# Seven-product pairs for three pairs of each output projection and for all of branch b's gate units, with branch a's last four units at the end of the attention

## The chip, the cores and the metric

The kernel runs on one core of one Trainium2 chip. The metric is device time in microseconds; of the kernel before, three runs gave a median of 880.55 us (879.84 to 883.31). The engines are named as in the profile: PE is TensorE's matmul, PEld its weight load, DVE is VectorE, ACT is ScalarE, POOL is GpSimd, SP is SyncE. A DMA is issued from the queue of SP or of POOL.

## The reference

Two layers of a decoder trunk on 512 tokens of 1024 channels, float32. What matters here:

```
h = rmsnorm(x);  u = h @ W_in             # columns: q, k, v, z of branches a, b, c; gates ga, gb, gc
ya, yb, yc = attention of 4 + 6 + 6 heads, each times silu(z)
merged = sigmoid(ga) * (ya @ w_br_a) + sigmoid(gb) * (yb @ w_br_b) + sigmoid(gc) * (yc @ w_br_c)
x = x + merged @ w_out                    # after two layers: a last rmsnorm
```

## The kernel before

**Data.** Activations lie transposed, channels on the 128 partitions and 512 tokens along the row, in eight tiles. For precision every operand is split in a high and a low part, and every product is three matmuls: high x high, low x high, high x low (`mm3`, L128). A *unit* is 128 output columns of a projection from 1024 inputs: 8 x 3 matmuls of 512 columns (`run_unit`).

**Weights.** A *chunk* is half a unit's weights (256 KB) or a branch projection's (192 KB). Its high part is loaded into a slot of ring `wh` (`RINGH`, 10 slots) by a DMA from POOL's queue (L1110); its low part is made in a slot of ring `wl` (`RING`, 7 slots) by a negation of the high part on ACT (L1139) and an accumulating DMA of the same block (L1140). Chunks that are sums of blocks (L1119) are cast on ACT (L1133) and subtracted on DVE (L1135), from raw blocks loaded by SP.

**A pair in seven products** (`pair_steps`). Two units are taken as a 2x2 block product in seven products of half the inputs and half the tokens (a scheme of Strassen and Winograd): 7 x 4 x 3 = 84 matmuls of 256 columns. Products 0, 1, 4 use plain blocks of the weights (forms `B11`, `B21`, `B22`), products 2, 3, 5, 6 use differences of blocks. Of the activations, four sums of tiles are needed, made once by `sums` (L601 to L611) and kept in the tiles of V (`vb`), of the probabilities (`P`) and in `PH`, `PL`. The products accumulate in PSUM banks `a`, `b`, `c`, read between the products by ACT and DVE.

**Order.** The program's text sets the order of items (`step` for TensorE's, `do` for the rest), loads and splits run ahead of them by the rings, and a planner then orders each engine's queue, except after `manual_schedule`, where the text's order holds. PSUM has three banks `mm` (units), four `att` (scores, transposes, products) and one `pv`.

**A layer.** V projections; then 17 rounds over 16 heads. Round h holds: transposes of head h-1 (L503), the items of slot `a<h>` of `plan`, the P x V product of head h-1 (L549), the scores of head h+1 (L438, L439), the items of slot `b<h>`. The slots hold the units of q, k, z and, as soon as branch a's outputs are there, gate units with their branch projection (`m_item`: 24 + 6 matmuls for branch a, 24 + 9 for b). Heads 0 to 3 are branch a's, 4 to 9 branch b's (scores over up to 512 keys, three banks), 10 to 15 branch c's (banded, two banks). A reduction on DVE (L472) reads each score block. After the rounds: units 2 and 3 of branch b alone, then six pairs (branch b from 4, all of c), then the output projection. In layer 0 it is eight single units (`o_item`), each followed by a step of the next layer's V projection (`v_item`); its results are added to x, stored, scaled and split (`split_x`), squared and summed (`square_sum`, additions on POOL). In layer 1 it is 16 half units (`last_item`, 24 matmuls of 256 columns, first all with the first 256 tokens), with the weights of all eight kept on chip; then the final norm of each half (`rms_pe`, `rms_root`, `store_half`).

Of the kernel before, what the change touches and what calls it, by code (L numbers as in the profile page):

```python
# [13 lines left out]
P = 128  # L14
S = 512
D = 1024
L = 2
# [10 lines left out]
RING = 7  # L28
RINGH = 10
# [35 lines left out]
def tile_trunk(ctx: ExitStack, tc: tile.TileContext, xT, wpk, gT, gfT, bfg, snk,  # L65
# [96 lines left out]
    def square_sum(x, k):  # L162
# [9 lines left out]
    def rms_pe(_, tbs=range(4), accs=("acc",)):  # L172
        ps = st["ss"] = pv_bank()
# [358 lines left out]
    def pv_item(l, h, pair):  # L532
# [64 lines left out]
    def sums(l, k):  # L597
        def run():
# [3 lines left out]
            u, v = tmp(), tmp()  # L602
            nc.vector.tensor_tensor(u[:, T0], a[:, T1], b[:, T1], op=ALU.add)
            nc.vector.tensor_tensor(u[:, T1], u[:, T0], a[:, T0], op=ALU.subtract)
            nc.vector.tensor_tensor(v[:, T0], a[:, T0], a[:, T1], op=ALU.subtract)
            nc.vector.tensor_tensor(v[:, T1], b[:, T0], u[:, T1], op=ALU.subtract)
            h, lo = sum_places(k)
            for n, w in ((0, u), (1, v)):
                c = slice(n * S, n * S + S)
                nc.scalar.copy(h[:, c], w)  # L610
                nc.vector.tensor_tensor(lo[:, c], w, rd(h[:, c]), op=ALU.subtract)  # L611
            st["SH", k], st["SL", k] = h, lo
        return run

# [31 lines left out]
    def pair_steps(l, br, i, last=False):  # L646
# [5 lines left out]

        def A(half, tok):
            return lambda k: (XH[k + 4 * half][:, tok], XL[k + 4 * half][:, tok])

        def Sm(m):
            c = slice((m - 1) * HT, m * HT)
            return lambda k: (st["SH", k][:, c], st["SL", k][:, c])

        def prod(bank, form, xf):  # L660
            def pe(HL):
                new = bank not in d
                if new:
                    d[bank] = att_bank()[:, :HT]
                wh, wl = HL[0]
                for k in range(4):
                    c = slice(k * P, (k + 1) * P)
                    xh, xl = xf(k)
                    mm3(d[bank], wh[:, c], wl[:, c], xh, xl, new and k == 0, k == 3,
                        bank != "c")  # L670
            step(pe, [("w", l, br, i, form)])
# [77 lines left out]
        prod("b", 2, Sm(1))  # L749
        do(now(e5))  # L750
        prod("a", 3, Sm(2))
# [4 lines left out]
        prod("b", 4, Sm(4))  # L756
        do(now(c12))
        prod("a", 5, Sm(3))
# [12 lines left out]
    def o_item(e):  # L771
        d = {}

        def pe(HL):
            if e == 0:
                load_res(0)
                load_res(1)
            d["ps"] = run_unit(HL, [st["MH", i] for i in range(8)], [st["ML", i] for i in range(8)], LATE)

        def post():  # L780
            x1 = tmp()
            nc.vector.tensor_tensor(x1, d["ps"], st["xr", e], op=ALU.add)
            if e + 2 < 8:
                load_res(e + 2)
            nc.sync.dma_start(x1d[:, e, :], x1)
            split_x(x1, 1, e)
            square_sum(x1, e)
        step(pe, [("o", 0, e, h) for h in range(2)])
        do(post)

    def load_half(n):
        hf, e = divmod(n, 8)
        t = st["xr", n] = T([P, S], F32, "sz", 2)[:, :HT]
        nc.sync.dma_start(t, x1d[:, e, hf * HT:(hf + 1) * HT])

    def last_item(hf, e):
        d = {}
        n = 8 * hf + e  # L800
        tok = slice(hf * HT, (hf + 1) * HT)

        def pe(HL):
            if n == 0:
                load_half(0)
                load_half(1)
            if hf == 0:
                st["WO", e] = HL
            ps = mm_bank()[:, :HT]
# [7 lines left out]
        def post():  # L817
            if hf == 0:
                st["X2", e] = T([P, S], F32, "mg", 8)
            x2 = st["X2", e][:, tok]  # L820
            nc.vector.tensor_tensor(x2, d["ps"], st["xr", n], op=ALU.add)
            if n + 2 < 16:
                load_half(n + 2)
            acc = f"acc{hf}"
            if e == 0:
                st[acc] = T([P, S], F32, "ys", 2)[:, :HT]
                nc.scalar.activation(st[acc], x2, AF.Square)
            else:
                sq = tmp()[:, :HT]
                nc.scalar.activation(sq, x2, AF.Square)  # L830
                if e < KT - 1:
                    nc.vector.tensor_tensor(st[acc], st[acc], sq, op=ALU.add)
                else:
                    st[f"sq{hf}"] = sq
            nc.scalar.activation(x2, x2, AF.Copy, scale=st["gf"][:, e:e + 1])
        step(pe, [("o", L - 1, e, h) for h in range(2)] if hf == 0 else ())
# [17 lines left out]
    def last_projection():  # L854
        h0, h1 = range(0, 2), range(2, 4)
        for e in range(8):
            last_item(0, e)
            if e == 6:
                do(root_warm)
        for e in range(8):  # L860
            last_item(1, e)
            if e == 1:
                step(lambda _: rms_pe(_, h0, ("acc0", "sq0")))
                do(lambda: rms_root(h0))
            if e == 3:
                step(lambda _: rbc_pe(_, h0))
                do(lambda: store_half(0))
        step(lambda _: rms_pe(_, h1, ("acc1", "sq1")))
# [407 lines left out]
```

## Time and profile before

| | |
|---|---|
| median of three runs | 880.55 us |
| the profiled execution | 884.22 us |
| its span | 882.5 us |
| TensorE busy | 865.5 us, 98% |
| VectorE, ScalarE, GpSimd busy | 64%, 58%, 50% |
| granted clock, mean | 0.994 |

The span is the time from the first to the last instruction of one profiled execution; the runs are timed without a profile. An engine's busy time is a union over its instructions, so pipelined matmuls don't count twice.

### The profile page before, as it was taken

To read this page: it belongs to the slowest core of one execution; us is meant where nothing else is said; L and a number is where in the kernel's file an instruction comes from. 1 tells how busy PE (TensorE), PEld (TensorE's weight loads), DVE (VectorE), ACT (ScalarE), POOL (GpSimd) and SP (SyncE) were. 2 spreads that over 40 slices of the span, in tenths; PEclk is the share of its full clock that TensorE was granted. 3 is DMA by queue.
4 is the path that set the end of the run, shared out by engine and by line. 5 is a ranking of instruction groups with operands and counts; after the bars stand their busy time and mean duration, and the time that the engine had idled before them with its cause. 6 is when DMAs were issued, how large, how long until landed. Compare 5 with 4: busy or idle time off the path is not lost.

```text
span 882.5 us, 14401 instructions
## 1 busy us (share of the span) xinstructions
PE 865.5 (98%) x4866; PEld 750.1 (85%) x4866; DVE 567.9 (64%) x1242; ACT 510.4 (58%) x1072; POOL 440.5 (50%) x570
## 2 busy tenths in 40 slices
PE   9999999999999999999999999999999999999995
PEld 6988888888888889987888888888888888999994
DVE  7446788577576767752124658967685858687633
ACT  7477567565655655554335856666465756556541
POOL 5354576655444254566654446666444434544301
PEclk9999999999999999999999999999999999999997
DMA  9697768978989799999997886888899897998413
GB/s 303 142 207 141 161 142 168 190 144 189 199 182 228 193 185 247 205 200 284 250 233 156 174 164 149 153 168 172 158 205 193 186 223 158 226 247 183 160 48 111
DMA packets 97082, 163.83 MB, mean 186 GB/s; under 512 B 12144, under 2 KB 26864, under 8 KB 97008
## 3 DMA queue, kind: packets, MB, share of 16 engines
q0 software_dynamic: 71424, 121.70, 69.2%
q1 hardware_dynamic: 25440, 41.20, 14.2%
q8 instruction: 38, 0.62, 0.3%
q14 instruction: 36, 0.29, 0.1%
q10 hardware_dynamic: 144, 0.01, 0.0%
HBM read 153.43 MB, written 4.19 MB: 179 GB/s over the span
## 4 chain that ended last, share of the span: by engine, by line
PE 76%; issue 7%; POOL 5%; DMA 5%; DVE 3%; ACT 2%; SPq 0%; POOLq 0%; DVEq 0%; ACTq 0%
PE mm L131 17%; PE mm L130 17%; PE mm L132 17%; PE att L130 3%; PE att L131 3%; PE att L132 3%; PE pv L549 3%; PE att L503 3%; POOL wl L1140 3%; POOL wh L1110 2%; PE att L439 2%; PE att L438 2%; PE att L234 1%; PE att L235 1%; PE att L233 1%
## 5 line engine op out<-in xcount | busy, mean ns | idle before, releaser
L1140 POOL DMA_DIRECT2D wl<-in_wpk_dram x248 | 224.7, 925 | 185.8 <-ACT wl L1139 157.0
L1110 POOL DMA_DIRECT2D wh<-in_wpk_dram x248 | 169.6, 693 | 175.4 <-PE mm L132 130.2
L1139 ACT ACTIVATE wl<-wh 128x512 fp32r<-128x512 f32 (+3 forms) x248 | 148.3, 602 | 141.7 <-PE mm L132 113.2
L130 PE MATMUL mm<-xh,wh 128*128 128x512 f32 x544 | 217.6, 400 | 0.0
L131 PE MATMUL mm<-xl,wh 128*128 128x512 f32 x544 | 214.5, 394 | 0.0
L132 PE MATMUL mm<-xh,wl 128*128 128x512 f32 x544 | 214.4, 394 | 0.0
L132 PEld LDWEIGHTS mm<-xh,wl 128*128 128x128 f32 x544 | 102.2, 188 | 24.1
L130 PEld LDWEIGHTS mm<-xh,wh 128*128 128x128 f32 x544 | 102.3, 188 | 22.2
L131 PEld LDWEIGHTS mm<-xl,wh 128*128 128x128 f32 x544 | 102.3, 188 | 22.1
L474 ACT ACTIVATE P<-P,ng 128x256 f32<-128x256 f32 (+3 forms) x128 | 67.0, 525 | 24.9 <-DVE ng L472 24.4
L130 PE MATMUL mm<-y,wh 128*128 128x512 f32 (+1 forms) x132 | 49.9, 378 | 1.2 <-ACT y L711 1.2
L529 DVE TENSOR_TENSOR PL<-att,PH 128x512 fp32r<-128x512 f32 (+2 forms) x84 | 46.1, 598 | 7.0 <-ACT PH L528 7.0
L131 PE MATMUL mm<-y,wh 128*128 128x512 f32 (+1 forms) x132 | 50.1, 379 | 0.3 <-DVE y L712 0.3
L132 PE MATMUL mm<-y,wl 128*128 128x512 f32 (+1 forms) x124 | 47.5, 383 | 0.0
L130 PE MATMUL att<-xh,wh 128*128 128x256 f32 x144 | 40.7, 282 | 0.0
L492 DVE TENSOR_SCALAR P<-P,den 128x256 f32<-128x256 f32 (+3 forms) x128 | 39.8, 376 | 1.0
L132 PE MATMUL att<-xh,wl 128*128 128x256 f32 x144 | 40.4, 281 | 0.0
L131 PE MATMUL att<-xl,wh 128*128 128x256 f32 x144 | 40.4, 281 | 0.0
L528 ACT CAST PH<-att 128x512 fp32r<-128x512 f32 (+2 forms) x84 | 38.8, 526 | 1.3 <-PE att L503 0.6
L439 PE MATMUL att<-qk,qk 128*128 128x256 f32 (+2 forms) x128 | 36.9, 308 | 0.0
L503 PE MATMUL att<-ident,P 128*128 128x128 f32 x284 | 36.2, 272 | 0.0
L438 PE MATMUL att<-qk,qk 128*128 128x256 f32 (+2 forms) x128 | 36.1, 308 | 0.0
(260 smaller groups left out, 2034.8 us busy)
## 6 DMA issues: line engine op xcount, KB each, us to landing
wh<-in_wpk_dram POOLq DMA_DIRECT2D x196, 256.0 KB, 4.7
wl<-in_wpk_dram POOLq DMA_DIRECT2D x196, 256.0 KB, 5.2
y<-in_wpk_dram SPq DMA_DIRECT2D x32, 256.0 KB, 5.5
qk<-in_wpk_dram SPq DMA_DIRECT2D x24, 256.0 KB, 4.8
wh<-in_wpk_dram POOLq DMA_DIRECT2D x32, 192.0 KB, 5.0
wl<-in_wpk_dram POOLq DMA_DIRECT2D x32, 192.0 KB, 4.4
tmp<-tmp SPq DMA_DIRECT2D x80, 64.0 KB, 4.0
mg<-in_xT_dram SPq DMA_DIRECT2D x8, 256.0 KB, 5.7
```

The lines of the kernel that those rows point to most:

```text
L130: nc.tensor.matmul(ps, wh, xh, start=first, stop=False, skip_group_check=part)
L131: nc.tensor.matmul(ps, wh, xl, start=False, stop=False, skip_group_check=part)
L132: nc.tensor.matmul(ps, wl, xh, start=False, stop=last, skip_group_check=part)
L438: nc.tensor.matmul(ps, q[:, qs], kh[:, a:a + n], start=True, stop=False)
L439: nc.tensor.matmul(ps, q2[:, qs], k2[:, a:a + n], start=False, stop=True)
L474: nc.scalar.activation(pb, pb, AF.Exp, bias=ng[:, i:i + 1], scale=-1.0, accum_out=den[:, i:i + 1])
L492: nc.vector.tensor_scalar(blks[i], blks[i], den[:, i:i + 1], None, op0=ALU.mult)
L503: nc.tensor.transpose(ps[:, c * P:(c + 1) * P], pt[:, src * P:(src + 1) * P], st["ident"])
L529: nc.vector.tensor_tensor(st["PL"][:, o:o + n], bk[:, :n], rd(hh), op=ALU.subtract)
L1110: nc.gpsimd.dma_start(hl[i][0][:, :w], ap)
L1139: nc.scalar.activation(lo[:, :w], rd(h[:, :w]), AF.Copy, scale=-1.0)
L1140: nc.gpsimd.dma_start(lo[:, :w], ap, accum_op=ALU.add)
```

## The change

It makes seven-product pairs of all eight gate units of branch b (four pairs a layer, before two) and of six of the eight output units of each layer. In layer 0 output units 0 and 1 stay single and the pairs (2,3), (4,5), (6,7) alternate with V steps; in layer 1 units 6 and 7 stay as half units, first tokens ahead of the pairs and last tokens behind them. Four sums of the merged tiles (`sums_m`, with the body of `sums` in `four_sums`) are made for them; product 6 goes to the bank of `pv`, and layer 1 loads its eight residual tiles into `xh`, `xl` (`residuals`). The squares of layer 0's projection are added on DVE (`side`). Branch a's gate units move later: 0 to 3 are spread over slots a6 to a14, 4 and 5 stand in the last slots and 6 and 7 behind the rounds, where branch b's units stood. The rings shrink, since two more tiles hold branch outputs. All pieces of layer 0's output pairs are split on chip from raw blocks (`is_split`).

```diff
-RING = 7
-RINGH = 10
+RING = 6
+RINGH = 8
...
-            eng = nc.vector if k == KT - 1 else nc.gpsimd
+            eng = nc.vector if k == KT - 1 else side
...
-                yh, yo = (y_slot((2 * pair + w) % 10) for w in range(2))
+                yh, yo = (y_slot(2 * pair + w) for w in range(2))
...
+    def four_sums(k, a, b):
+        u, v = tmp(), tmp()
+        nc.vector.tensor_tensor(u[:, T0], a[:, T1], b[:, T1], op=ALU.add)
+        nc.vector.tensor_tensor(u[:, T1], u[:, T0], a[:, T0], op=ALU.subtract)
+        nc.vector.tensor_tensor(v[:, T0], a[:, T0], a[:, T1], op=ALU.subtract)
+        nc.vector.tensor_tensor(v[:, T1], b[:, T0], u[:, T1], op=ALU.subtract)
+        h, lo = sum_places(k)
+        for n, w in ((0, u), (1, v)):
+            c = slice(n * S, n * S + S)
+            nc.scalar.copy(h[:, c], w)
+            nc.vector.tensor_tensor(lo[:, c], w, rd(h[:, c]), op=ALU.subtract)
+    def sums_m(k):
+        return lambda: four_sums(k, st["M", k], st["M", k + 4])
...
+    def o_pair(l, e, bank, res, finish):
+        def add(u, tok, b, first):
+            def run():
...
+                other = st["xr", e + u] if first else x[u]
+                nc.vector.tensor_tensor(x[u][:, tok], d[b], other[:, tok], op=ALU.add)
+                if not first:
+                    finish(e + u, x[u], tok)
+            return urgent(run) if l + 1 < L else run
+        res(e)
+        prod("a", 0, M(0, T0))
+        do(add(0, T0, "a", True))
+        prod("c", 1, M(1, T0))
+        do(add(0, T0, "c", False))
+        prod("b", 2, sum_part(1))
+        do(add(1, T1, "b", True))
+        prod("a", 3, sum_part(2))
+        do(add(1, T0, "a", True))
+        prod("b", 4, sum_part(4))
+        do(add(1, T0, "b", False))
+        prod("a", 5, sum_part(3))
+        do(add(1, T1, "a", False), add(0, T1, "a", True))
+        prod("e", 6, M(1, T1))
+        do(add(0, T1, "e", False))
+    def first_projection():
...
+        do(lambda: load_res(0), lambda: load_res(1), sums_m(0))
+        o_item(0)
+        do(sums_m(1))
+        o_item(1)
+        do(sums_m(2), sums_m(3))
+        o_pair(0, 2, mm_bank, res, finish)
+        v_item(1, 0)
+        v_item(1, 1)
+        o_pair(0, 4, mm_bank, res, finish)
+        v_item(1, 2)
+        v_item(1, 3)
+        o_pair(0, 6, mm_bank, res, finish)
+        for k in range(4, 8):
+            v_item(1, k)
...
     def last_projection():
+        do(residuals, sums_m(0), sums_m(1))
+        last_item(T0, 6)
+        do(root_warm, sums_m(2))
+        last_item(T0, 7)
+        do(sums_m(3))
+        for e in (0, 2, 4):
+            o_pair(1, e, att_bank, lambda e: None, finish)
+        do(lambda: ctx.enter_context(tc.manual_schedule()))
+        step(lambda _: rms_pe(_, h0, ("acc0", "sq0"), att_bank))
+        do(lambda: rms_root(h0))
+        last_item(T1, 6)
+        step(lambda _: rbc_pe(_, h0))
+        do(lambda: store_half(0))
+        last_item(T1, 7)
...
-            "b5": [(0, 0)], "a6": [(0, 1)], "b7": [(0, 2)], "b8": [("qc", 1, 12)], "a9": [("qc", 2, 14)],
-            "b9": [(0, 3)], "a10": [(0, 4)], "b10": [("zc", 0, 5)], "a11": [(0, 5)], "b11": [],
-            "a12": [(0, 6)], "a14": [("zc", 2, 7)], "a15": [(0, 7)], "a16": [(1, 0)], "b16": [(1, 1)],
+            "b5": [], "a6": [(0, 0)], "b7": [], "b8": [], "a9": [("qc", 1, 12)],
+            "b9": [], "a10": [(0, 1)], "b10": [], "a11": [("zc", 0, 5)], "b11": [("qc", 2, 14)],
+            "a12": [(0, 2)], "a14": [(0, 3)], "a15": [("zc", 2, 7)], "a16": [(0, 4)], "b16": [(0, 5)],
...
-        solo(M(1, 2))
+        solo(M(0, 6))
         do(sums(l, 1))
-        solo(M(1, 3))
-        for br, i in ((1, 4), (1, 6), (2, 0), (2, 2), (2, 4), (2, 6)):
+        solo(M(0, 7))
+        for br, i in ((1, 0), (1, 2), (1, 4), (1, 6), (2, 0), (2, 2), (2, 4), (2, 6)):
...
+    def is_split(key):
+        return is_plain(key) or key[0] == "w" and (key[4] in SUMS or key[1:3] == (0, 3))
```

The slots of `plan` stand here several to a line; slots that are not named keep what they hold.

## Rows read from the trace of the kernel before

**Rows 1.** The page, parts 1 and 2: busy time; 40 slices in tenths.
```profile
PE 865.5 (98%) x4866; PEld 750.1 (85%) x4866; DVE 567.9 (64%) x1242; ACT 510.4 (58%) x1072; POOL 440.5 (50%) x570
...
PEclk9999999999999999999999999999999999999997
DMA  9697768978989799999997886888899897998413
```

**Rows 2.** TensorE's waits: engine, line, releaser: us in total, times, longest.
```profile
PE att L130 <- ACT tmp L721: 2.8, 2, 1.5
...
PE mm L130 <- ACT y L711: 1.2, 2, 0.7
```

**Rows 3.** Stretches: length; busy (count) of PE, PEld, DVE, ACT, POOL; clock, DMA share, GB/s.
```profile
282.20:305.17 22.97, 22.97 (x102) 18.59 (x100) 16.62 (x33) 14.43 (x26) 9.46 (x14) 1.00 0.91 217
319.61:333.71 14.10, 14.10 (x103) 13.31 (x102) 9.12 (x16) 7.12 (x15) 7.09 (x10) 1.00 0.95 191
390.29:391.71 1.42, 1.42 (x13) 1.42 (x12) 0.33 (x1) 1.05 (x2) 1.11 (x3) 1.00 1.18 264
431.92:437.47 5.55, 5.55 (x25) 4.50 (x24) 0.00 (x0) 1.23 (x2) 3.65 (x5) 1.00 0.96 231
822.05:851.93 29.88, 28.88 (x243) 28.48 (x242) 15.23 (x29) 17.30 (x35) 7.77 (x6) 1.00 0.30 94
```

**Rows 4.** Timeline at transposes and scores: start, us, engine, line, op, out<-in, count.
```profile
149.48 1.25 PE L503 MATMUL att<-ident,P 128*128 128x128 f32 x10
150.49 0.48 PE L130 MATMUL mm<-xh,wh 128*128 128x512 f32 x1
...
142.52 0.39 PE L130 MATMUL mm<-xh,wh 128*128 128x512 f32 x1
...
143.46 0.07 DVE L472 DVE_READ_ACCUMULATOR2_ANT ng<- 128x1 f32 x1
143.94 0.07 DVE L472 DVE_READ_ACCUMULATOR2_ANT ng<- 128x1 f32 x1
...
174.89 0.39 PE L130 MATMUL mm<-xh,wh 128*128 128x512 f32 x1
...
175.91 0.08 DVE L472 DVE_READ_ACCUMULATOR2_ANT ng<- 128x1 f32 x1
177.09 0.07 DVE L472 DVE_READ_ACCUMULATOR2_ANT ng<- 128x1 f32 x1
```

**Rows 5.** Timeline of one chunk of a gate pair: negation, accumulating DMA, first use.
```profile
331.82 0.53 ACT L1139 ACTIVATE wl<-wh 128x384 fp32r<-128x384 f32 x1 [0.64 <-PE att L132]
...
332.64 0.87 POOL L1140 DMA_DIRECT2D wl<-in_wpk_dram  x1
...
340.79 0.40 PE L130 MATMUL mm<-y,wh 128*128 128x512 f32 x1
```

**Rows 6.** Gate pairs, 305 to 391: tiles wl, then wh; ScalarE's waits.
```profile
DMA to landing us min/median/max: 3.5/5.1/7.4
...
DMA to landing us min/median/max: 3.0/5.6/7.7
...
ACT wl L1139 <- DMA wh<-in_wpk_dram: 7.1, 6, 1.8
```

**Rows 7.** Timeline of VectorE in the sums: two of 256 columns, two of 512.
```profile
305.66 0.41 DVE L605 TENSOR_TENSOR tmp<-tmp 128x256 f32<-128x256 f32 x1
306.00 0.41 DVE L606 TENSOR_TENSOR tmp<-tmp,tmp 128x256 f32<-128x256 f32 x1
306.33 0.68 DVE L611 TENSOR_TENSOR vb<-tmp,vb 128x512 fp32r<-128x512 f32 x1
306.94 0.68 DVE L1135 TENSOR_TENSOR wl<-qk,wh 128x512 fp32r<-128x512 f32 x1
```

**Rows 8.** The stretch in which the first projection's sums would be made.
```profile
388.39:407.00 18.61, 18.11 (x82) 14.21 (x81) 7.58 (x13) 8.81 (x17) 12.51 (x18) 1.00 1.12 254
```

**Rows 9.** Timeline of VectorE: scaling half of the output, at the end.
```profile
874.45 2.08 DVE L851 TENSOR_TENSOR tmp<-pv,mg 128x256 f32<-128x256 f32 x6 [1.30 <-ACT rbc L841]
```

More of the change, by code (lines that the diff above doesn't have):

```diff
@@ L160, in split_x, with square_sum @@
                                            op0=ALU.mult, op1=ALU.subtract)
-    def square_sum(x, k):
+    def square_sum(x, k, side=nc.gpsimd):
         if k == 0:
@@ L601, in run, with part, sum_part, products @@
                 nc.scalar.activation(t, t, AF.Copy, scale=g_sb[:, l, kk:kk + 1])
[L602 to L612, printed above, removed]
-        return run
+            four_sums(k, a, b)
+        return run
+    def four_sums(k, a, b):
[9 more added lines that the diff above has]
+            nc.vector.tensor_tensor(lo[:, c], w, rd(h[:, c]), op=ALU.subtract)
+        st["SH", k], st["SL", k] = h, lo
+    def sums_m(k):
+        return lambda: four_sums(k, st["M", k], st["M", k + 4])
+    def part(hs, ls, half, tok):
+        return lambda k: (hs[k + 4 * half][:, tok], ls[k + 4 * half][:, tok])
+    def sum_part(m):
+        c = slice((m - 1) * HT, m * HT)
+        return lambda k: (st["SH", k][:, c], st["SL", k][:, c])
+    def products(key, d, new_bank):
+        def prod(bank, form, xf):
+            def pe(HL):
+                new = bank not in d
+                if new:
+                    d[bank] = (pv_bank if bank == "e" else new_bank)()[:, :HT]
+                wh, wl = HL[0]
+                for k in range(4):
+                    c = slice(k * P, (k + 1) * P)
+                    xh, xl = xf(k)
+                    mm3(d[bank], wh[:, c], wl[:, c], xh, xl, new and k == 0, k == 3, bank not in "ce")
+            step(pe, [key + (form,)])
+        return prod
     def m_item(l, br, i):
@@ L651, in pair_steps @@
         now = urgent if br == 2 else (lambda fn: fn)
+        prod = products(("w", l, br, i), d, att_bank)
         def A(half, tok):
[L654 to L671, printed above, removed]
+            return part(XH, XL, half, tok)
         def branch(u):
@@ new lines, in first_projection, with res, run, finish @@
+    def first_projection():
+        def res(e):
+            def run():
+                for u in range(2):
+                    if e == 4:
+                        t = T([P, S], F32, "sz", 2)
+                    else:
+                        t = y_slot(8 + u, F32)
+                    st["xr", e + u] = t
+                    nc.sync.dma_start(t, xT[:, e + u, :])
+            do(run)
+        def finish(e, x1, tok):
+            if tok == T0:
+                return
+            nc.sync.dma_start(x1d[:, e, :], x1)
+            split_x(x1, 1, e)
+            square_sum(x1, e, nc.vector)
+        do(lambda: load_res(0), lambda: load_res(1), sums_m(0))
[12 more added lines that the diff above has]
+            v_item(1, k)
@@ new lines, in quarter @@
+    def quarter(e, x, tok, last):
+        hf = int(tok == T1)
+        x2 = x[:, tok]
+        acc = f"acc{hf}"
+        if acc not in st:
+            st[acc] = T([P, S], F32, "ys", 2)[:, :HT]
+            nc.scalar.activation(st[acc], x2, AF.Square)
+        else:
+            sq = tmp()[:, :HT]
+            nc.scalar.activation(sq, x2, AF.Square)
+            if last:
+                st[f"sq{hf}"] = sq
+            else:
+                nc.vector.tensor_tensor(st[acc], st[acc], sq, op=ALU.add)
+        nc.scalar.activation(x2, x2, AF.Copy, scale=st["gf"][:, e:e + 1])
```

164 lines of the change are left out of this document (66 added, 98 removed).

## The prediction

> **What bounds the kernel now.** I read the page first, then TensorE's waits, then tables of stretches cut at the first matmul of an item, and last the timelines of the places that the change touches. [rows 1] TensorE is busy 98% of 882.5 us, in every slice, with its clock granted in full (2.4 GHz), while VectorE stands at 64%. [rows 2] Its longest waits are 2.8 and 1.2 us in total, so no other engine holds it: the kernel lasts as long as TensorE's work, plus the start and the tail. Two questions follow: how much TensorE work goes, and which engines, covered today, are covered no longer.
>
> **What is removed.** [rows 3] Three single units of branch b (99 matmuls of 512 columns) take 22.97 us, 7.66 each and 15.31 for two. A pair in seven products with its two branch projections takes 14.10. One product (12 matmuls of 256 columns) takes 1.42, a single output unit (24 of 512) 5.55, a half output unit (24 of 256) twice 1.42, or 2.84.
> - Branch b: units 0 to 3 of each layer become two pairs, so four pairs in all: 4 x (15.31 - 14.10) = 4.8 us.
> - First output projection: three pairs, 3 x (2 x 5.55 - 7 x 1.42) = 3 x 1.16 = 3.5 us.
> - Last output projection: its units run as halves already, so a pair replaces four halves: 3 x (4 x 2.84 - 9.94) = 4.3 us.
> - [rows 3] The last stretch, 240 matmuls, takes 29.88 us where 20 x 1.42 = 28.4 are needed: it waits 1.5 us for the last merged channels; such waits stand in [rows 2]. After the change the first halves there need only the first 256 tokens, which are merged earlier; I count 1.3 (0 to 1.5).
> Sum 13.9 us. Branch a's last units move and cost the same 30 matmuls each.
>
> One rule speaks against all of this. The rows give 0.118 us a matmul of 256 columns and 0.231 of 512: halving the width halves the time. The Trainium skill (TensorE: Matmul & The Clock Gate, "Back-to-back issue gap") has about 81 ns sustained for 128 columns and 131 for 512; an estimate from that page for 256 is some 98 ns, by which seven products (84 x 98 = 8.2 us) would cost 1.9 us more than the 48 wide matmuls (6.3 us) and the change would lose some 10 us. The trace disagrees on both widths, so this rule gets no chance.
>
> **What is added.** Five costs; none of them is matmul work.
>
> (a) Attention, thinner cover. Per layer the sixteen heads lose two units of branch a and two of branch b, so slots b5, b7, b8, b9 and b10 are empty while heads 4 to 9 still use three score banks and three transpose banks out of four. With nothing between the scores of head h+1 and the transposes of head h, the second transpose bank waits for the second reduction and the third for the third. [rows 4] Ten transposes take 1.01 us. Scores that end at 142.52 have their second reduction done at 143.53 and the third at 144.01: 0.4 us of transposes, 0.6 of waiting, 0.4, then 0.1; 0.7 us lost. Scores that end at 174.89 have theirs at 175.99 and 177.16: 0.7 + 0.8 = 1.5 us. Three such places a layer (b5, b7, b8; at b9 and b10 the next head needs two banks): six in all, 4.2 to 9.0 us. The lower end is 0: the planner may put the next unit's matmuls, which wait for nothing, ahead of the transposes. I take 2.5, a little over half of 4.2.
>
> (b) Weight rings, low parts 7 to 6, high parts 10 to 8. [rows 5] A low part in the pairs is made by a negation on ScalarE (331.82), an accumulating DMA issued 0.8 us later (332.64) and used at 340.79, 9.0 us after the negation, which starts when the slot comes free. [rows 6] The DMA lands after 5.1 us in the median and 7.4 at most: the chain needs 5.9, at most 8.2. With six slots the negation starts five chunks before the use: 7.1 us where these are five products, 7.8 to 8.4 where branch projections of (14.10 - 9.94) / 2 = 2.08 are among them. So only the slowest landings are late, by 1.1 us. In 16 pairs I count one or two: 1.5 us. Bounds 0 (fewer transfers in flight may land sooner) and 16, worked out under the rivals.
>
> (c) Sums for the first projection. The three pairs need four sums of the merged channels: 16 VectorE operations of 256 columns and 8 of 512. [rows 7] Back to back these start 0.34 and 0.60 us apart, so 4 x 2.56 = 10.2 us. From the last gate pair's second branch projection (388.39) to the last sum's use is 3.3 us to the end of that pair, 11.1 of two single units, 2.84 of two products and 1.06 of the third: 18.3 us, about the stretch to 407. [rows 8] VectorE is busy 7.6 of 18.6 us there and has 11.0 free. New in it: sums 10.2, splits of the first four forms 3.6, a squares addition that was GpSimd's 0.6, two additions 0.7: 15.1, less 2.7 for the first two sums' additions, which need channels merged a pair earlier. That is 12.4 in 11.0: 1.4 late, of which 0.2 may hide; I take 1.2. Bounds 0 (matmuls of the next layer's v units put ahead) and 5 (nothing done early, and an us of waits for ScalarE between).
>
> (d) Sums for the last projection. Here only two half units (5.68) precede the products: from the same point 3.5 + 5.68 + 2.84 + 1.06 = 13.1 us. VectorE owes the last pair's merging (4.1), sums 10.2, splits of two forms 2.4, two residual additions with their squares 1.0, two additions 0.7: 18.4 - 2.7 = 15.7, 2.6 late. Behind them the three pairs give no recovery: each asks VectorE for 8 x 0.60 + 12 x 0.34 = 8.9 us in 9.94. And ScalarE casts between the steps. I take 3.3; bounds 1 (additions and later splits put off) and 8 (a tenth of VectorE's 40 us here lost to in-order waits, and the residuals, now loaded only when their slots come free after the last gate product, late).
>
> (e) Tail. The first half's scaling now lies between the last two half units. [rows 9] Six products take 2.08 us; with the addition, square and accumulation of the unit before them (1.6 us after its last matmul) they end 3.7 us after that matmul, where the last unit's addition could start at 3.2: 0.4 us. Bounds 0 and 1.5, the latter if the root's chain is late too.
>
> Sum added 2.5 + 1.5 + 1.2 + 3.3 + 0.4 = 8.9. Net -5.0. The profiled execution took 884.22 us, 1.8 of them around its span, and would take 879.2; it lies 3.67 above the median of the runs, 880.55, so the forecast there is **875.5 us**.
>
> What costs nothing: fewer bytes move in the first projection (a pair's four blocks are loaded once and split on chip); [rows 1] the DMA engines stay the busiest thing beside TensorE in the gate pairs, as before. SP's loads of raw blocks stand ahead of the residuals in program order, so the residuals wait, not the weights.
>
> **Rivals.**
> - **The waits stay hidden.** The planner fills (a) and (c) with other matmuls, the rings hold, (d) costs its lower bound. For it: [rows 2] today's order leaves hardly any wait in 880 us. Against: in the last projection no other matmul is ready. 13.9 - 0.4 - 1.0 = 12.5 saved: 868.0 us.
> - **VectorE becomes the bound in both projections**: (c) 5 and (d) 8, the rest as forecast: 17.4 added, +3.5: 884.0 us. For it: the demand over the last projection (18.4 and 3 x 8.9 against 39 us of TensorE's) is above the time. Against: [rows 8] half of VectorE's time at this place is free today.
> - **The rings decide, and it gets slower.** A high part's slot is held from its load to its last matmul: [rows 6] 5.6 to land, 0.8, 5.1, then 1.42 of use, 12.9 us. A pair uses nine chunks in 14.10, 1.57 each: ten slots give 15.7 us, eight give 12.5. Short by 0.4 in eight chunks, 0.45 a pair, 7.2 in 16 pairs; with a slowest landing in every second pair 8 x 1.1 = 8.8: 16.0 for (b) instead of 1.5. +9.5: 890.0 us. It decides from the point where a slot's tour is longer than eight chunks. For it: [rows 6] ScalarE already waits 7.1 us in six waits for high parts to land, with ten slots. Against: four of nine chunks are cast from blocks on chip and hold their slots shortly.
>
> **How the numbers follow.** Forecast 0.45 (its own range 872 to 880), hidden waits 0.24, VectorE 0.20, rings 0.11. The range runs from 867, where nothing but the smallest of the costs is left, to 889, which leaves out most of the ring case's far side. What a measurement of this kernel can tell is some 0.5%, 4.4 us, so faster is below 876.1: all of the hidden case and over half of the forecast, 0.48. Slower is above 885.0: the rings and a part of VectorE's case, 0.19. Same 0.33.
>
> **What would show it.** After the change TensorE's busy time falls by 12 to 13 us; pairs of units take 9.9 us in the projections and 14.1 in branch b. Waits of TensorE on VectorE at the transposes of heads 5, 7 and 8, and at the third product of the first pair of each projection, show (a), (c) and (d); waits on an accumulated weight in the gate pairs show (b). The prediction is wrong if those at the third products are absent, if gate pairs are longer than 14.5 us, or if TensorE's idle time exceeds 25 us.

## The result, and the profile after

The changed kernel takes 945.51 us (median of 4 runs, 943.73 to 949.96) against 880.69 for the kernel before on the same chip: a ratio of 1.074, 95% interval 1.069 to 1.078, so 65 us slower. The forecast was 875.5, its range ended at 889. The profiled execution took 943.73 us, its span 942.0. One execution of a kernel of the experiments, e4, took 4820 us where its other three took about 910; the times given for it leave that one out.

The page of the changed kernel, the lines of [rows 1]:
```profile
PE 877.3 (93%) x5082; PEld 760.5 (81%) x5082; DVE 644.1 (68%) x1423; ACT 537.1 (57%) x1132; POOL 418.1 (44%) x550
...
PEclk9999999999999999989999999999999999999898
DMA  8497777679999899875497877775798998889862
```
TensorE now idles 65 us of the span, 17 before. Its busy time was to fall by 12 to 13 us and rose by 11.8; the lower clock explains some 10 of that difference (last section), the rest wasn't traced. Its longest waits, the view of [rows 2]:
```profile
PE att L132 <- DMA wl<-in_wpk_dram: 17.1, 19, 2.1
PE att L503 <- DVE ng L472: 6.2, 4, 3.0
PE mm L132 <- DMA wl<-in_wpk_dram: 5.6, 6, 1.8
PE att L130 <- DVE tmp L751: 4.9, 1, 4.9
PE att L130 <- ACT P L614: 3.4, 1, 3.4
PE att L234 <- DMA wl<-in_wpk_dram: 3.0, 1, 3.0
```
Low parts (wl) that the accumulating DMA hasn't delivered, the attention's transposes (L503), and the sums of the third product (L614) all show now. Where the time went is read from the stages, with the columns of [rows 3]: attention, gate pairs and first projection of layer 0, then attention, gate pairs and last projection of layer 1. Before:
```profile
41.78:305.17 263.39, 263.39 (x1318) 221.30 (x1316) 182.50 (x431) 166.09 (x366) 139.41 (x177) 1.00 0.85 182
305.17:391.71 86.54, 84.99 (x613) 79.74 (x612) 62.18 (x112) 48.30 (x95) 46.14 (x66) 1.00 0.94 199
391.71:459.69 67.98, 67.48 (x290) 53.93 (x289) 15.39 (x24) 26.98 (x45) 44.11 (x58) 1.00 1.09 256
472.42:735.75 263.33, 263.33 (x1318) 221.18 (x1317) 183.25 (x431) 166.08 (x367) 139.62 (x177) 1.00 0.86 180
735.75:822.05 86.30, 84.97 (x613) 79.75 (x612) 64.44 (x114) 47.88 (x95) 40.08 (x54) 1.00 0.91 206
822.05:873.90 51.85, 48.71 (x406) 47.82 (x404) 24.15 (x58) 24.47 (x52) 9.21 (x8) 0.98 0.27 87
```
After:
```profile
42.54:283.07 240.53, 235.42 (x1185) 195.87 (x1184) 174.18 (x423) 159.65 (x355) 123.80 (x155) 1.00 0.82 174
283.07:412.45 129.38, 118.28 (x817) 108.05 (x816) 81.27 (x147) 59.26 (x119) 57.34 (x80) 0.99 0.89 198
412.45:489.32 76.87, 68.28 (x398) 57.91 (x397) 52.74 (x101) 35.86 (x62) 20.09 (x29) 0.96 0.68 163
503.04:743.40 240.36, 235.70 (x1185) 197.08 (x1183) 172.77 (x422) 158.08 (x353) 123.27 (x155) 0.99 0.80 172
743.40:877.67 134.27, 118.57 (x818) 108.31 (x817) 83.04 (x151) 61.44 (x124) 61.34 (x87) 0.98 0.91 206
877.67:934.00 56.33, 48.18 (x369) 46.24 (x368) 43.45 (x105) 31.44 (x66) 11.11 (x16) 0.95 0.57 149
```
The attention lost four units of 7.66 us, so 232.7 were due and each takes 8 more. Eight gate pairs at the 14.4 us each of before are 115: they take 14 and 19 more. The first projection was due at 68.0 - 3.5 = 64.5 and takes 12 more; the last with its tail at 51.9 - 5.6 = 46.3 and takes 10 more. No stage gained what it was to gain.

Behind the gate pairs stands ScalarE: its negations now wait for high parts to land (the line of [rows 6], over the whole span; the kernel before, then the changed one):
```profile
ACT wl L1139 <- DMA wh<-in_wpk_dram: 13.2, 12, 1.8
...
ACT wl L1219 <- DMA wh<-in_wpk_dram: 105.4, 44, 5.4
```
The longest, 5.4 us, falls on the start of the first projection. Timeline of ScalarE and VectorE there (start, length, engine, line, what, and idle time before with its releaser):
```profile
415.58 0.63 ACT L1219 ACTIVATE wl<-wh 128x512 fp32r<-128x512 f32 x1 [5.37 <-DMA wh<-in_wpk_dram]
416.12 1.12 ACT L614 CAST vb<-tmp 128x512 fp32r<-128x512 f32 x2
...
416.75 1.29 DVE L615 TENSOR_TENSOR vb<-tmp,vb 128x512 fp32r<-128x512 f32 x2 [5.49 <-ACT vb L614]
...
419.40 0.62 ACT L725 CAST y<-mg 128x512 fp32r<-128x512 f32 x1 [1.63 <-DVE mg L714]
```
One negation waits for one landing. Behind it in ScalarE's order stand the sums' casts; VectorE idles 5.5 us for those, adds up the last merged channels only after them, and ScalarE casts these at 419.40, while TensorE waits. Two-microsecond stretches of the same place (columns as above):
```profile
414.00:416.00 2.00, 1.87 (x9) 1.17 (x7) 0.00 (x0) 0.42 (x1) 0.00 (x0) 1.00 1.08 272
416.00:418.00 2.00, 0.33 (x1) 0.30 (x2) 1.25 (x3) 1.77 (x4) 1.42 (x2) 1.00 1.08 298
418.00:420.00 2.00, 0.88 (x4) 0.38 (x2) 1.66 (x4) 0.60 (x2) 0.00 (x0) 0.70 1.11 241
420.00:422.00 2.00, 1.93 (x3) 0.78 (x3) 1.95 (x5) 1.36 (x4) 0.00 (x0) 0.50 0.52 145
422.00:424.00 2.00, 1.52 (x4) 1.12 (x4) 1.97 (x5) 0.75 (x2) 0.00 (x0) 0.50 0.00 0
424.00:426.00 2.00, 2.00 (x7) 1.58 (x6) 2.00 (x6) 1.29 (x3) 0.00 (x0) 0.59 0.12 44
```
After some 3 us with little to do TensorE's clock stands at 0.50 (1.2 GHz) until 424 and later, and most of the wait is paid a second time.

### The profile page after: what moved, and what is told of

It reads as the page before. It is cut to its first block, busy times and chain, and to the rows that moved or that the text cites. A ratio compares the mean times of both kernels' runs of the same rounds, so it can differ in the third digit from the quotient of the medians.

```text
span 942.0 us, 15134 instructions
## 1 busy us (share of the span) xinstructions
PE 877.3 (93%) x5082; PEld 760.5 (81%) x5082; DVE 644.1 (68%) x1423; ACT 537.1 (57%) x1132; POOL 418.1 (44%) x550
## 4 chain that ended last, share of the span: by engine, by line
PE 46%; DMA 18%; issue 14%; POOL 9%; DVE 7%; ACT 4%; SPq 1%; POOLq 0%; DVEq 0%; ACTq 0%
PE mm L130 10%; PE mm L132 10%; PE mm L131 10%; DMA wh<-in_wpk_dram 7%; DMA wl<-in_wpk_dram 6%; POOL wl L1220 5%; POOL wh L1189 4%; PE att L503 3%; PE pv L549 3%; DMA tmp<-tmp 3%; PE att L132 2%; PE att L130 2%; PE att L131 1%; PE att L438 1%; PE att L439 1%
## 5 line engine op out<-in xcount | busy, mean ns | idle before, releaser
L1219 ACT ACTIVATE wl<-wh 128x512 fp32r<-128x512 f32 (+3 forms) x241 | 143.4, 600 | 199.3 <-DMA wh<-in_wpk_dram 105.4
L130 PE MATMUL mm<-xh,wh 128*128 128x512 f32 x480 | 193.1, 402 | 0.0
L132 PE MATMUL mm<-xh,wl 128*128 128x512 f32 x480 | 190.5, 397 | 0.0
L131 PE MATMUL mm<-xl,wh 128*128 128x512 f32 x480 | 189.9, 396 | 0.0
L132 PE MATMUL att<-xh,wl 128*128 128x256 f32 x192 | 57.0, 297 | 14.8 <-DMA wl<-in_wpk_dram 14.7
L131 PE MATMUL att<-xl,wh 128*128 128x256 f32 x192 | 54.7, 285 | 0.0
L132 PEld LDWEIGHTS att<-xh,wl 128*128 128x128 f32 x192 | 37.2, 194 | 18.3 <-DMA wl<-in_wpk_dram 18.1
L503 PE MATMUL att<-ident,P 128*128 128x128 f32 x284 | 38.9, 275 | 8.9 <-DVE ng L472 6.2
L130 PE MATMUL att<-vb,wh 128*128 128x256 f32 x152 | 43.8, 288 | 1.8 <-ACT tmp L735 1.6
L503 PEld LDWEIGHTS att<-ident,P 128*128 128x128 f32 x284 | 32.3, 141 | 15.9 <-issue 9.1
L132 PE MATMUL att<-vb,wl 128*128 128x256 f32 x152 | 43.5, 286 | 1.7 <-DMA wl<-in_wpk_dram 1.7
L130 PE MATMUL mm<-y,wh 128*128 128x512 f32 (+1 forms) x106 | 41.9, 395 | 1.7 <-ACT y L725 1.7
L131 PE MATMUL att<-vb,wh 128*128 128x256 f32 x152 | 43.2, 284 | 0.0
```

Of the source, the lines that this page charges most:

```text
L130: nc.tensor.matmul(ps, wh, xh, start=first, stop=False, skip_group_check=part)
L131: nc.tensor.matmul(ps, wh, xl, start=False, stop=False, skip_group_check=part)
L132: nc.tensor.matmul(ps, wl, xh, start=False, stop=last, skip_group_check=part)
L503: nc.tensor.transpose(ps[:, c * P:(c + 1) * P], pt[:, src * P:(src + 1) * P], st["ident"])
L1219: nc.scalar.activation(lo[:, :w], rd(h[:, :w]), AF.Copy, scale=-1.0)
```

## The experiments

Each kernel was timed beside the kernel before (882 to 884 us in these sessions); ratios are to that, with 95% intervals. "Six and eight" are six low and eight high slots.

**Rings.** e1, the kernel before with the change's rings; e2 and e3, the changed kernel with one slot more:
```
e1:  RING = 7, RINGH = 10  ->  RING = 6, RINGH = 8     (kernel before)
e2:  RING = 6              ->  RING = 7                (changed kernel)
e3:  RINGH = 8             ->  RINGH = 9               (changed kernel)
```


> The kernel before with the change's rings alone: six slots for low parts instead of seven, eight for high parts instead of ten; all else as before (the last projection's resident weights that lose their ring slots get tiles of their own in the freed space). Theory DMA (my own now): in the gate pairs the 16 DMA engines have more to move than time. Per pair 2.36 MB on GpSimd's queues at 18.62 MB in 72.2% of 129.38 us (199 GB/s) and 1.05 MB on SyncE's at 6.82 MB in 16.0% (329 GB/s): 11.8 + 3.2 = 15.0 us of all engines, 16.0 at the 0.94 share that the gate pairs of before reach, against 14.1 of TensorE. Then the rings only set how much is loaded ahead: losing two high and one low parts costs at most 3 x 1.3 = 4 us a layer, so 881 to 889. Rival, rings: a slot's tour sets the pace and the changed kernel's 2.0 to 2.7 us per gate pair come from the smaller rings; the twelve pairs of before lose as much: 25 us or more, 905.

> The changed kernel with seven low slots again (high parts stay at eight). Rings theory: the low parts are what TensorE waits for in its gate pairs (16.1 us in 17 waits in the two layers), so with the slot back at least half of the 38 us go: 927 or less. DMA theory: the engines still have 16 us of work per pair; one chunk more of reserve is worth 1.5 us a layer: 941 to 946.

> The changed kernel with nine high slots (low parts stay at six). Rings theory with the high slot's tour (12.9 us against eight chunks 12.5; nine give 14.1): the pace recovers, 38 us go but for some: 915. DMA theory: one chunk of reserve, 1.5 us a layer: 941 to 946.

Measured: e1 915.04 us (1.036, 1.034 to 1.039), e2 1018.21 (1.152), e3 921.58 (1.042). My theory, bytes, fell three times: e1 lost 33 us where 881 to 889 us was forecast, and one slot more costs 73 us in the low ring and gives 24 in the high one. e1's gate pairs and first projection of layer 0:
```profile
308.62:402.74 94.12, 87.04 (x613) 79.84 (x612) 61.10 (x110) 46.02 (x93) 42.97 (x61) 1.00 0.84 177
402.74:477.01 74.27, 71.02 (x291) 55.72 (x290) 15.74 (x24) 27.31 (x46) 45.63 (x60) 0.95 1.05 238
```
Against 86.54 and 67.98 before, with a DMA share that is lower, not higher (0.84 against 0.94). ScalarE's wait for high parts in e1, whose rings differ by two, and in e2, where they differ by one:
```profile
ACT wl L1140 <- DMA wh<-in_wpk_dram: 80.0, 37, 3.7
...
ACT wl L1219 <- DMA wh<-in_wpk_dram: 295.8, 137, 6.5
```
In e3, with a difference of three, it is 23.5 us. So I formed a second theory, lead: only the difference of the rings counts, since the negation is issued that many chunks behind its load.
```
e5:  RING = 6  ->  RING = 5                      (changed kernel)
e6:  RING = 7  ->  RING = 6                      (kernel before)
e9:  RING = 7, RINGH = 10 -> RING = 6, RINGH = 9 (kernel before)
```


> The changed kernel with five low slots instead of six, so less room, but three chunks instead of two between the load of a high part and its negation (eight less five). Theory lead: the negations stand in ScalarE's order and wait for a high part that was asked for only as many chunks earlier as the two rings differ; a chunk is 1.57 us in the gate pairs, a landing 5.8 us, so two chunks (3.1 us) make nearly every negation wait and three (4.7 us) few. Sums of these waits so far: difference three 13.2 us (before) and 23.5 (six and nine), two 105.4 (the change) and 80.0 (before with six and eight), one 295.8 (seven and eight). So ScalarE's wait on high parts falls from 105 to 20 to 35 us and the time to 921, as with six and nine; 915 to 932 since five low slots leave the accumulation 6.3 us instead of 7.8. Rival, capacity: fewer slots are worse, and what helped with nine was the slot: 950 to 965.

> The kernel before with six low and ten high slots: difference four. Theory lead: the 13.2 us of ScalarE's waits on high parts go nearly to nothing; TensorE hardly waited for them, so 878 to 884, no loss from the low slot. Rival, capacity of the low parts (the step of the prediction in which the low part with six slots is late in one pair of eight, 1.5 us to 16 us): 884 to 898, with waits of TensorE on accumulated low parts of 4 us and more.

> The kernel before with six low and nine high slots, the rings that the run of the two projections alone had. Theory capacity (a high part's slot is held for its landing, the negation, the accumulation and its product; the number of high slots sets the pace, and the low slots how much of that is left to the accumulation): between six and eight (915.0) and six and ten (891.2): 900, 895 to 906. Then of the 28 us by which the projections alone were slower (910.5 against 882.5), some 17 are the rings' and 11 the projections' own. Rival, lead (only the difference of the rings counts, three as before): 882 to 886, and all 26 are the projections'.

Measured: e5 955.94 (1.083), e6 891.20 (1.009, 1.007 to 1.011), e9 891.42 (1.009). Lead is right for ScalarE's wait on high parts, which goes by the difference of the rings: 295.8 us at one, 105.4 and 80.0 at two, 13.2 (before), 23.5 (e3), 13.9 (e9) and 7.0 (e5) at three. As a rule for the time it fell: e5 has the difference of three and is worse than the change; its negations hardly wait any more, but TensorE waits for low parts:
```profile
PE mm L132 <- DMA wl<-in_wpk_dram: 22.0, 13, 3.8
```
What fits all of them is capacity: a high slot is held through both transfers, the two rings divide that time between load and accumulation, and eight slots are too few in each division tried (956, 946 and 1018 us with five, six and seven low ones). On the kernel before the last low slot is worth 9 us, the tenth high slot nothing beside six low ones, the ninth 24; for nine I had forecast 895 to 906 by capacity, and they do as well as ten.

Two rivals weren't tried. Two separate needs, six low slots and a difference of three, fit these eight kernels as well as nine high slots do; seven low and nine high would tell them apart. And GpSimd issues loads and accumulations in one order, so a late landing can make the next loads late too, as here in the gate pairs of the changed kernel:
```profile
303.55 0.63 ACT L1219 ACTIVATE wl<-wh 128x512 fp32r<-128x512 f32 x1 [3.10 <-DMA wh<-in_wpk_dram]
...
304.48 0.85 POOL L1220 DMA_DIRECT2D wl<-in_wpk_dram  x1 [3.56 <-ACT wl L1219]
305.03 1.42 POOL L1189 DMA_DIRECT2D wh<-in_wpk_dram  x2
```
The negation waits 3.1 us for its landing, the accumulation 3.6 us for the negation, and two loads stand behind that. How much of the loss is this circle and how much the slots, no run separates.

**Fewer bytes.** e4: the plain forms of the pairs are split on the chip. e7: the same with nine high slots. e12: the same as e7 with GpSimd subtracting. e10: that on the kernel before.
```
-    return is_plain(key) or key[0] == "w" and (key[4] in SUMS or key[1:3] == (0, 3))
+    return is_plain(key) or key[0] == "w"
e12, e10 also:
+    eng = nc.gpsimd if key[0] == "w" and key[4] not in SUMS else nc.vector
```


> The changed kernel, but the three forms of each pair that are plain quarters (first, second and fifth product) are split on the chip from the raw blocks that are loaded anyway, as the first projection's pairs do it, instead of being loaded twice more from memory. Per pair 1.57 MB less on GpSimd's queues; three more subtractions of 0.68 us on VectorE. DMA theory: 0.79 MB at 199 GB/s and 3.2 us are 7.1 us of engines a pair, far under 14.1: the gate pairs go back to 14.2 and lose 30 to 35 us, and the late negation that blocks ScalarE at the first projection's start (5.4 us, then a lower clock) goes too: 905, 900 to 912. Rival, VectorE: it is busy 81.3 of 129.4 us there and gets 16 more in 113: 86%, in-order waits then hold pairs at 14.8 or more: 912 to 925. If neither holds and latency, not bytes, was the cause, nothing changes for the branch units' parts: 930.

> The changed kernel with six and nine slots and all seven forms of each pair split on the chip from the raw blocks. Theory lead: both steps take ScalarE's waits on high parts away, the nine slots in the attention and the branch units, the split in the pairs: below both 921.6 (nine slots alone) and 911.0 (split alone): 897, 890 to 905; ScalarE's wait on high parts under 20 us. Rival, VectorE: three more subtractions a pair make it late in the gate pairs, which then stand at 14.8 us and more: 906 to 915.

> The run with six and nine slots and all forms split on the chip (909.5), with the three plain forms' subtractions on GpSimd instead of VectorE. If VectorE holds the gate pairs there (14.46 and 14.7 us a pair) and the projections' starts, it gets 8 x 3 x 0.68 = 16 us a layer back: 902, 898 to 906. Rival: what is left are the attention's empty slots and the late raw blocks of the first output pair, which block ScalarE ahead of the last merged channels' cast: 907 to 911.

> The kernel before (rings seven and ten), but in the gate pairs the three forms that are plain quarters are split on the chip from the raw blocks that are there, a cast on ScalarE and a subtraction on GpSimd (1.30 us in the last projection's rows), instead of two transfers of 0.26 MB each that GpSimd issues (0.69 and 0.93 us). Theory: the weights' supply is the gate pairs' limit even before (14.42 us a pair against 14.10); with 1.57 MB a pair less it is not: 12 x 0.3 = 3.7 us less, and somewhat less waiting behind it: 877, 873 to 880. Rival: these waits were not the supply's, or GpSimd's subtractions come late behind its other work: 881 to 888.

Measured: e4 910.44 (1.030), e7 909.50 (1.030), e12 921.51 (1.044), e10 892.71 (1.011). e4 moves the time as expected, but after e1 to e3 that doesn't speak for bytes alone: a form split on the chip has no chain of two transfers, so its slot is held shortly. In e7 the ninth slot adds next to nothing more, for a reason that wasn't settled; on GpSimd the subtraction costs 1.6 us, not the 1.30 I had reckoned with (group of e10; busy and mean ns behind the bar):
```profile
L1137 POOL TENSOR_TENSOR wl<-y,wh 128x512 fp32r<-128x512 f32 x18 | 28.9, 1611 | 2.6 <-DVE wl L1137 1.2 <-PE att L132 1.1 <-DVE tmp L724 0.2
```
e10's forecast was wrong in sign. Its gate pairs of layer 0 move far less than before and take 1.3 us longer:
```profile
306.70:394.53 87.83, 85.82 (x613) 79.99 (x612) 76.29 (x115) 47.02 (x95) 49.08 (x52) 1.00 0.51 108
```
So fewer bytes alone didn't give the 0.3 us a pair back; what GpSimd's longer subtractions cost beside that wasn't taken apart.

**The parts by themselves.** e8: the two projections alone (attention and branch b as before), rings six and nine. e13: the same with seven and ten. e11: e10 with branch b's two pairs, branch a left in the attention.
```
e8, e13:  plan, solos (1, 2), (1, 3) and pairs from (1, 4) as in the kernel before
e13:      y_slot(2 * pair + w) -> y_slot((2 * pair + w) % 10);  RING, RINGH = 7, 10
e11:      "a16": [], "b16": [], no solos;  pairs (1, 0), (1, 2), (1, 4), ...
```


> The two projections of the change alone: branch b's first four units one by one and branch a's units in the attention as in the kernel before; rings of six and nine. If attention and branch b cost what the stages of the run with six and nine show (attention 8.7 us a layer above its matmuls, gate pairs 9.0 and 7.7, projections 12.2 and 6.0, against 1.4 to 1.9 a stage before), this kernel keeps the projections' part alone: 882.3 - 7.8 - 1.3 + 12.2 + 6.0 + about 3 for the low slot and the tail = 894, 888 to 900. Rival: the projections' losses were brought in from the gate pairs (late weights that block ScalarE as the projection begins), which are shorter here: 877 to 884.

> The two projections of the change alone, as in the run with six and nine (910.5), with the old rings of seven and ten (branch c's first channels share tiles with branch a's again, which makes the room). Rings theory: 8.9 us less, as on the kernel before (891.4 to 882.5): 901, so the projections cost 19 us by themselves. Rival, latency: what the projections lose comes from the rings too (weights late at their start), then 880 to 892.

> The run before with branch b's first four units in two pairs of seven products as well; branch a's units stay in the attention, the two slots at the attention's end stay empty, the projections stay as before. TensorE's work falls by 4.8 us. Without four single units as cover the sums of the first pair (some 10 us of VectorE a layer, of which the last head's work covers about half) show: 5 us a layer, so 877 + 10 - 4.8 = 882, 877 to 888. Rival, supply: eight pairs in a row drain the loads, 2 us a pair as in the changed kernel: 890 to 900.

Measured: e8 910.49 (1.031), e13 901.34 (1.020, 1.016 to 1.023), e11 911.35 (1.032). The projections cost 19.1 us at equal rings of six and nine (e8 less e9; 20.6 if each is first compared with the kernel before beside it) and 18.4 with the old rings. e3 less e8 is the price of the attention and branch b: 11.1. e11 shows why branch a's units were put at the attention's end: without them the sums of the first pair stand bare,
```profile
PE att L130 <- ACT vb L610: 15.3, 2, 7.7
```
and the kernel is 18.6 us slower than e10, these waits included.

**The start of the projections.** e14 and e15 hold back the first output pair's casts and negations behind the last merged channels, e14 with the planner, e15 in the written order; both on e13. e16 is e15 with the last projection's part alone.
```
split_to:
+   if key[0] == "w" and key[2] == 3 and ptr["used"] <= where[last]: return
e14:  last = ("w", l, 2, 6, 6)      e15, e16:  last = ("o", l, 6 * l, 1)
e15, e16:  tc.manual_schedule() from the last gate pair on (layer 0: to o_item(1))
```


> The run before, but no form of an output pair is cast or negated until the last branch product has been issued, so that on ScalarE the casts of the last merged channels come first. Theory, ScalarE's order: TensorE's waits on those casts (2.1 and 4.1 us in the run with six and nine) go, and the lower clock that follows them; 6 to 10 us less than the run before: 893. Rival: the casts were late for the merges' own sake, or the pairs' weights are now as much later as the channels are earlier: within 3 us of the run before.

> The two projections alone with the old rings (901.3), but the order of the last gate pair and of the two units behind it is the written one, without the planner, and no form of the first output pair is cast ahead of the last merged channels. Theory, ScalarE's and VectorE's order: TensorE's wait of 3 us on the last merged channels' cast (ScalarE's cast of the pair's raw block and VectorE's subtraction behind it wait for the block's landing, and the channels' last addition stands behind these), and the half clock after it, go in the first projection: 4 to 7 us less, 895. Rival: the pair's weights then come as much later as the channels come earlier, or the written order costs elsewhere what it gives here: 899 to 906.

> The last projection's part of the change alone (first projection as in the kernel before), old rings, with the written order in the last gate pair and behind it. By the stages of the run with both projections the last layer gave 3.8 us away in the gate pairs and 4.8 in the last projection with its tail, the first layer 8.7 in its projection less 1.9 in its gate pairs: 882.5 + 8.6 = 891, less up to 4 if the order is at fault: 887 to 892. Rival: the last layer's losses came from the first projection's (late weights carried on), then 878 to 884, and this is a faster kernel.

Measured: e14 902.68 (1.021), e15 918.87 (1.040), e16 904.98 (1.024). In e14 the planner still put the first cast, which waits for its raw block, ahead of the channels' last addition. In e15 the written order held, and the place itself healed: the 48 matmuls of the first two single units take
```profile
389.81:400.91 11.10, 11.10 (x50) 9.02 (x49) 6.85 (x15) 3.92 (x7) 0.55 (x1) 1.00 0.91 280
```
where e13 took 16.65. But the weights that were held back are then late, in the last projection by more than was won:
```profile
PE att L132 <- DMA wl<-in_wpk_dram: 10.6, 1, 10.6
```
So the order is a cause at that place and no cure: my reading is that channels and weights compete for one ScalarE in a stretch too short for both. e17 and e18 ask for the raw blocks only at the third form, so that the first two forms load ahead (e17 on e13, e18 the last projection's part alone):
```
-   if is_plain(key) or key[0] == "w" and key[4] == 0:
+   if is_plain(key) or key[0] == "w" and key[4] == (2 if key[1:3] == (1, 3) else 0):
...
-   busy[tag] = i + (0 if name is None else 6 if key[2] == 3 else 8)
+   busy[tag] = i + (0 if name is None else (4 if key[1] else 6) if key[2] == 3 else 8)
```


> The two projections alone with the old rings and the planner's order (901.3), but in the last projection a pair's raw blocks are asked for at its third form, the first that needs them, not at its first: the high parts of the first two forms no longer wait for the raw blocks' slots. Theory, supply: from the last branch product to the first pair's first product TensorE has 1.4 + 5.7 us of other work, the chain behind it load 5.6, negation 0.8, accumulation 5.1; with the first two forms loaded ahead it is over in time. The last layer's gate pairs and last projection, 146.8 us together against 138.2 before, come down by 5 to 8: 895. Rival, sums: the casts and subtractions of the four sums (the waits on the third product, 3.4 us) or the raw blocks for the third form set the start: 899 to 903.

> The last projection's part alone, with the same later raw blocks, planner's order, old rings; first projection as in the kernel before. Theory, supply: the last layer gives no more than 1 to 3 us away against before: 882 to 886; faster than before only if the waits at the start go wholly: then down to 878. Rival, sums and in-order VectorE: 889 to 893, as the last layer's 8.6 us of the run with both say.

Measured: e17 902.52 (1.022), e18 893.46 (1.011, 1.009 to 1.013). The supply of the first two forms isn't it. e18, with first projection and rings as before, is 10 us slower where 5.6 were to be won. Two places of it, columns as above:
```profile
818.00:820.00 2.00, 1.66 (x8) 1.02 (x6) 0.00 (x0) 0.00 (x0) 1.93 (x3) 1.00 1.17 219
820.00:822.00 2.00, 0.00 (x0) 0.00 (x0) 0.81 (x3) 0.92 (x2) 0.85 (x2) 1.00 1.01 200
...
824.00:826.00 2.00, 2.00 (x12) 2.00 (x11) 2.00 (x5) 0.61 (x1) 0.00 (x0) 0.50 1.10 265
...
838.00:840.00 2.00, 0.00 (x0) 0.00 (x0) 2.00 (x6) 1.43 (x3) 1.11 (x2) 0.86 0.45 51
...
842.00:844.00 2.00, 1.49 (x6) 1.19 (x6) 2.00 (x5) 1.67 (x3) 0.23 (x1) 0.50 0.97 326
```
From 818 to 820 VectorE and ScalarE stand still behind one late landing (TensorE then waits 3.3 us for a gate's addition); from 838 to 844 VectorE is full with sums and splits (the wait on the third product, 3.4 us). Behind each, TensorE runs some 6 us at 0.50. No version tried beats the kernel before, and seven (e2, e8, e10, e11, e12, e15, e16) are slower than both their forecast and the rival set against it.

## Why the prediction was wrong

The three parts add up. Rings alone (e1) 32.7, projections alone (e13) 18.4, attention and branch b (e3 less e8) 11.1: 62.2 of the 64.8 us, though each part was taken with other rings. The prediction had 1.5, -4.2 and -2.3.

- **Step (b) failed, and most.** I had put the rings' change at 1.5 us, bounds 0 to 16, with "only the slowest landings are late". It is 32.7. The step followed the low part alone, from a negation that starts when its slot comes free, and took the high part as landed. With eight and six slots its load is asked for only two chunks ahead, and the negation waits: 80.0 us in e1 against 13.2 before. What stands behind it, on ScalarE and in GpSimd's queue, waits too. The rival "the rings decide" had the side and, as it seems, the threshold: a tour of 12.9 us, against 12.5 for eight slots and 14.1 for nine. Its price, 7.2 + 8.8 us in 16 gate pairs, was too low, since each late slot was to cost its own delay alone and only the gate pairs were counted: e1 loses 7.6 and 10.1 us in 12 gate pairs, 6.3 in the first projection and 4.3 in the two attentions. My "against", that four of nine chunks hold their slots shortly, left out that the same ScalarE casts these four; no run tries that by itself.
- **Steps (c) and (d) sized their own wait about rightly and left out what comes before it.** At the third product TensorE waits 0.8 us in the first projection of the changed kernel and 3.9 in the last, against 1.2 and 3.3. Left out were the last merged channels, cast behind the first output pair's weights (e15 gives 5.5 us back at that place), and the lower clock behind each wait. By e13's stages, first projection, then gate pairs and last projection of layer 1,
```profile
391.16:467.84 76.68, 67.66 (x398) 58.68 (x397) 51.62 (x100) 34.27 (x60) 20.73 (x30) 0.96 0.66 168
744.10:834.12 90.02, 85.63 (x613) 80.05 (x612) 61.44 (x113) 48.18 (x95) 47.78 (x67) 1.00 0.95 207
834.12:890.80 56.68, 48.95 (x369) 47.49 (x368) 43.75 (x106) 31.32 (x64) 9.74 (x13) 0.92 0.63 167
```
layer 0 lost 12.2 us against 1.2, bounds 0 to 5, and layer 1 14.1 (3.7 in its gate pairs, 10.4 behind) against 3.3 + 0.4, bounds 1 to 8 and 0 to 1.5. In the first projection TensorE waits 3.7 us for the cast channels and 5.2 for low parts of v units, and the lower clock (0.96 in the mean, so some 6 us at 1.2 GHz) costs about 3 as an estimate. What the wait on the low parts rests on wasn't tried. The rival "VectorE becomes the bound in both projections" thus had the sign and half the size; VectorE is seen full only in the last projection.
- **Step (a) had the mechanism and was too small.** The waits stand at the transposes of heads 5, 7 and 8, as forecast (3.3 us in layer 0; in layer 1 3.0, all at head 7). At equal rings, e3 with the four units' 30.64 added against e8, the attention is 7.0 us longer in layer 0 and 3.1 in layer 1; e3's and e8's layer 0:
```profile
42.35:283.84 241.49, 235.46 (x1186) 196.14 (x1184) 173.51 (x423) 158.64 (x353) 123.62 (x155) 1.00 0.82 173
...
42.60:307.70 265.10, 264.41 (x1318) 220.97 (x1316) 181.53 (x431) 166.17 (x367) 142.34 (x179) 1.00 0.86 183
```
That is 10.1, above the 9.0 at the upper end; I took 2.5 on the hope that the planner fills the slots. It slips two or three matmuls in, and a wait remains, as at head 5 in the changed kernel:
```profile
147.52 0.85 PE L503 MATMUL att<-ident,P 128*128 128x128 f32 x6 [1.29 <-DVE ng L472]
```
- **What was removed was right.** Where nothing is late, the work still takes what [rows 3] say: the six gate pairs of layer 0 in e13 84.60 us, TensorE busy throughout, a product of the changed kernel, 411.05 to 412.45 us, 1.40. No run shows the price of narrow matmuls that the prediction had worked out from the Trainium skill (TensorE: Matmul & The Clock Gate, "Back-to-back issue gap"). The half clock was in no step.

One reading in passing was wrong too: between the waits of 2.8 and 1.2 us that the prediction took from [rows 2] as the longest stand two of 1.5 and 1.3 us. It changes nothing.

By its own tests the prediction called itself wrong: gate pairs above 14.5 us (16.2 and 16.8) and TensorE idle above 25 us (65).

## What to carry to other kernels

A high part's slot was held here through two transfers in a row, so count the whole tour against slots times the pace before giving one up, with the lead that each ring leaves its transfer, and expect a cliff: beside six low slots the tenth high slot was worth nothing, the ninth 24 us. A wait on a transfer in an in-order engine's stream is paid by all that stands behind it, so ask of each prefetch step which urgent work it stands ahead of. A saving on TensorE that is bought with more work for the other engines at a seam between stages should be priced at that seam, clock included.

## What was not expected of the hardware

In the changed kernel TensorE's clock fell five times before the tail, each time after one or two waits, 2.0 to 4.9 us together. Over stretches of 2 us, each counted by its granted clock, TensorE was busy 19.6 us at 1.2 GHz, 0.6 before; at half speed that is, as an estimate, some 10 us of the 65. The Trainium skill (TensorE: Matmul & The Clock Gate, "HAM oscillation — how this bites in real kernels") says that a stall on a DMA puts the array back to the slower clock, and the trace agrees: 1.00 before the idle stretch at 416 to 419 us, 0.50 after it. Here waits on VectorE and ScalarE did the same, 4.9 us on a gate's addition in layer 1 for one.

GpSimd's subtraction of 128x512 took 1.29 us in the last projection of before and 1.61 in the gate pairs of e10; why wasn't tried.
